# Two weight-split instructions pinned into a later place in their queues, at the end of the second block's output projection

## The chip, the cores and the metric

One core of a Trainium2 chip runs the whole program: two transformer blocks on 256 tokens of width 1024, batch 1, everything in fp32. The metric is the device time of one execution in microseconds (us); the number that counts is the median of the runs. Engines are named as in the profile: PE is TensorE, DVE is VectorE, ACT is ScalarE, POOL is GpSimd, SP is SyncE, which issues the loads.

## What is computed

The reference is two blocks in a row. The change lies in the second one, between its mixing part and its feed-forward part:

```python
mix = gates[:, :, 0] * y_attn + gates[:, :, 1] * y_pool + gates[:, :, 2] * y_mem
x = x + rms_norm(mix @ w_out[l], norm_mix_post[l])

h2 = rms_norm(x, norm_ffn_pre[l])
up = causal_depthwise_conv(h2 @ w_up[l], conv_w[l], conv_b[l])
g, v = jnp.split(up, 2, axis=-1)
ff = (jax.nn.gelu(g, approximate=True) * v) @ w_down[l]
x = x + rms_norm(ff, norm_ffn_post[l])
```

So after `mix @ w_out` each token row is normalised, added to `x`, normalised again, and only then can it meet `w_up`.

## The kernel before

**Products.** Every fp32 product is made of three: each operand is split into a high part `hi` (rounded to the matmul's format) and a remainder `lo`, and `mm3` (L205 to L208) sums hi·hi, hi·lo and lo·hi. In `b_part`, the form used here, the three matmuls on lines 206, 207 and 208 are x-hi with weight-hi, x-hi with weight-lo, x-lo with weight-hi, in this order.

**Weights.** All weights pass through one stream. A granule of 1 MB is loaded into one of three raw buffers (`feed`, L123) and is split in two halves by `split_next` (L129 to L151): ACT writes the half's `wh` by a cast (L142), then DVE, or POOL for one half that is marked so, writes `wl` by a subtraction (L143). There are six buffers of `wh` and six of `wl`; a half's buffers come free when PE has done the last matmul with it (`release`), a raw buffer when both halves' `wl` are written. `pump` splits one half ahead after each unit; `part` (L161 to L165) splits a half when its unit is reached and it isn't yet there.

**Order.** Only PE's queue follows the program text (`tc.manual_schedule` for PE). The queues of ACT, DVE, POOL and SP are ordered by the compiler's planner: an instruction that is not ready by the plan is passed by one that is. Each queue then runs in its order on the chip.

**The stage.** `out_stage` with `lead` set computes `mix @ w_out_2`. Tokens are two tiles of 128 rows, called t0 and t1 here; output columns are two halves, n0 and n1; w_out_2 is eight weight halves, four for n0 and four for n1. The last part is written out in `end_stage` and `close`:

- `first` (L505): `close(0)` does t0 with n1's four weight halves, splitting the last of them if need be; then t0's `finish`: add to `h`, squares on ACT, `pow` on POOL (L297), times the gain, and `scale` (L469 to L471), which multiplies x's columns 0 to 511 on DVE (L470) and the others on ACT (L471).
- `second` (L511): `close(1)` does t1 with n0's last two weight halves and n1's four. Ahead of the last of these it calls `turn` for t0: eight transposes on PE (L337), then `split_to`, which writes x^T's `hi` on ACT (L325) and `lo` on DVE (L326), in two column halves. Then comes t1's `finish`, with its own `scale`.
- `lead(0)` and `lead(1)` (L1307 on): the first matmuls with `w_up`, done in the row form so that they can start with one token tile. `lead(0)` takes t0 through six weight halves, called p0 to p5 here (`g_lead[0]` to `g_lead[2]`); t1's `turn` stands between p4 and p5. `lead(1)` takes t1 through the same six. p3's `wl` is on POOL, all others' on DVE.

No half of w_out_2 is left to be split after `close(0)`. So the first call of `split_next` after either `finish` is the one in `lead(0)` for p0. Behind p0 to p5, the next granule of the stream is the first of the feed-forward's own (p6, p7), which takes the raw buffer of p0 and p1.

Of the kernel before, what the change touches and what calls it, by code (L numbers as in the profile page):

```python
# [10 lines left out]
F32 = mybir.dt.float32  # L11
# [4 lines left out]
ALU = mybir.AluOpType  # L16
AX = mybir.AxisListType

P = 128
# [7 lines left out]
HALVES = (slice(0, 512), slice(512, D))  # L27
# [12 lines left out]
def two_blocks(ctx: ExitStack, tc: tile.TileContext, a: dict, out: bass.AP):  # L40
# [23 lines left out]
    V, S, G, PE = nc.vector, nc.scalar, nc.gpsimd, nc.tensor  # L64
# [3 lines left out]
    def nm(base):  # L68
        uid[0] += 1
        return f"{base}_{uid[0]}"  # L70
# [10 lines left out]
    XT, MT, ME = (xh, xl), (mh, ml), (eh, el)  # L81
# [7 lines left out]
    def s_t():  # L89
        return psum.tile([P, 512], F32, tag="s", name=nm("s"), bufs=4)  # L90
# [10 lines left out]
    def r32(ap):  # L101
        return ap.bitcast(F32R)
# [14 lines left out]
    def feed():  # L117
        while at_dma[0] < len(stream) and at_split[0] >= 2 * (at_dma[0] - N_RAW + 1):
            g = stream[at_dma[0]]
            g.raw = wraw.tile([P, g.nk, g.ncol], F32, tag="w", name=nm("w"))  # L120
            src = g.src.rearrange("(k p) c -> p k c", p=P)
            if at_dma[0]:
                nc.sync.dma_start(g.raw, src)  # L123
            else:
                for c in (slice(0, P), slice(P, 2 * P)):
                    nc.sync.dma_start(g.raw[:, :, c], src[:, :, c])
            at_dma[0] += 1

    def split_next(pieces=None, low=V):  # L129
        g, i = stream[at_split[0] // 2], at_split[0] % 2  # L130
        if g.by_col:
            c = g.ncol // 2
            src, shape = g.raw[:, :, i * c:(i + 1) * c], [P, g.nk, c]
        else:
            k = g.nk // 2
            src, shape = g.raw[:, i * k:(i + 1) * k, :], [P, k, g.ncol]
        hi = wspl.tile(shape, F32R, tag="wh", name=nm("wh"))
        lo = wspl.tile(shape, F32R, tag="wl", name=nm("wl"))
        g.parts[i] = (hi, lo)
        at_split[0] += 1  # L140
        if pieces is None:
            S.copy(hi, src)  # L142
            low.tensor_tensor(lo, src, hi.bitcast(F32), op=ALU.subtract)  # L143
        else:
            k = g.nk // 2
            for p in (np.s_[:, 0:k, :], np.s_[:, k:, :]):
                def piece(p=p):
                    S.copy(hi[p], src[p])
                    G.tensor_tensor(lo[p], src[p], hi[p].bitcast(F32), op=ALU.subtract)
                pieces.append(piece)  # L150
        feed()  # L151

    def pump(lead=N_SPLIT - 1):
        if at_split[0] < 2 * len(stream) and at_split[0] < n_used[0] + lead:
            split_next()

    def part(g, i, low=V):
        while g.parts[i] is None:
            assert at_split[0] < n_used[0] + N_SPLIT
            split_next(low=low)  # L160
        return g.parts[i]  # L161

    def release():
        n_used[0] += 1

    def place(fn, gran=None, pieces=()):

        if gran is not None:
            stream.append(gran)
        prog.append((fn, list(pieces)))  # L170
# [66 lines left out]
    def b_part(w, xt, t, k0, o, first, last):  # L237

        tok = slice(t * P, (t + 1) * P)
        for k in range(2):  # L240
            mm3(o, r32(xt[0][:, k0 + k, tok]), r32(xt[1][:, k0 + k, tok]), w[0][:, k, :], w[1][:, k, :],
                first and k == 0, last and k == 1)
# [24 lines left out]
    def ev_to(dst, scale=None):  # L267
        def ev(i, o):
            if scale is None:
                V.tensor_copy(dst, o)  # L270
            else:
                S.mul(dst, o, scale)
        return ev

    def grid(w, c0, n, dst, scale=None, xt=XT):

        u = []
        for g in range(n):
            u += a_units(cols(w, c0, g), xt, ev_to(dst[:, g * 512:(g + 1) * 512], scale))
        return u  # L280
# [40 lines left out]
    def split_to(dst, sl, src, scale=None):  # L321

        hi, lo = dst
        if scale is None:
            S.copy(r32(hi[sl]), src)  # L325
            V.tensor_tensor(r32(lo[sl]), src, hi[sl], op=ALU.subtract)  # L326
        else:
            S.activation(r32(hi[sl]), src, AF.Copy, scale=scale)
            V.scalar_tensor_tensor(r32(lo[sl]), src, scale, hi[sl], op0=ALU.mult, op1=ALU.subtract)  # L329

    def turn_rows(xn, t, dst, tile=tp_t):

        for c in range(2):
            o = tile()
            for k in range(4):
                kk = 4 * c + k
                PE.transpose(o[:, k * P:(k + 1) * P], xn[:, kk * P:(kk + 1) * P], ident)  # L337
            split_to(dst, np.s_[:, 4 * c:4 * c + 4, t * P:(t + 1) * P],
                     o.rearrange("p (k t) -> p k t", k=4))


    def turn_causal(pm):
# [48 lines left out]
    class Heads:  # L391


        def __init__(self, score, turn, pv):
            self.f, self.p, self.t = (score, turn, pv), {}, {}
# [17 lines left out]
    class Tail:  # L413
# [22 lines left out]
        def scale(self, dst, r):  # L436
            for n in range(2):
                V.tensor_scalar(dst[:, HALVES[n]], self.x[:, HALVES[n]], r[:, 0:1], None, op0=ALU.mult)
# [12 lines left out]
            self.scale(self.x, self.r)  # L451

        def turn(self):
            turn_rows(self.x, self.t, XT)

    class BlockEnd(Tail):

# [5 lines left out]
    class PostNorm(Tail):  # L463
# [3 lines left out]
            self.sum_times(self.o[n], n)  # L467

        def scale(self, dst, r):  # L469
            V.tensor_scalar(dst[:, HALVES[0]], self.x[:, HALVES[0]], r[:, 0:1], None, op0=ALU.mult)  # L470
            S.mul(dst[:, HALVES[1]], self.x[:, HALVES[1]], r[:, 0:1])  # L471

        def add(self, c):
# [22 lines left out]
    def end_stage(tails, close, fill, lead=None):  # L496


        def first():
            for _ in range(2):  # L500
                pump(N_SPLIT)
            close(0)()
            tails()[0].finish()

        def second():  # L505
            close(1)()
            tails()[1].finish()

        do(first)
        do(second)  # L510
        if lead is not None:  # L511
            lead(0, lambda: tails()[1].turn())
            lead(1, None)
        else:
            run(fill, {2 * t: [lambda t=t: tails()[t].turn()] for t in range(2)})

    def out_stage(src, xt, tail, gains, fill=(), at=None, lead=None):

        at = at or {}
        held = (2, 3) if lead is not None else ()  # L520
        st = {}
        gr = {(n, kq): Granule(src[kq * 512:(kq + 1) * 512, HALVES[n]], 4, 512, False)
              for n in range(2) for kq in range(2)}

        def unit0(i):
            if i == 0:
                st["o"] = [[s_t(), s_t()] for _ in range(2)]
                st["g"] = gains()
                st["tails"] = [tail(t, st["o"][t], st["g"]) for t in range(2)]
            w = part(gr[0, i // 2], i % 2)  # L530
            for t in range(1 if i in held else 2):
                b_part(w, xt, t, 2 * i, st["o"][t][0], i == 0, i == 3)
            if i not in held:
                release()
            if i == 3:
                for t in range(1 if held else 2):
                    st["tails"][t].half(0)

        for i in range(4):
            place(lambda i=i: unit0(i), gr[0, i // 2] if i % 2 == 0 else None, at.get(i, ()))  # L540
        stream.extend(gr[1, kq] for kq in range(2))

        def close(t):
            def go():
                for n, j in ([(0, j) for j in held] if t else []) + [(1, j) for j in range(4)]:
                    if held and (t, n, j) == (1, 1, 3):
                        st["tails"][0].turn()
                    b_part(part(gr[n, j // 2], j % 2), xt, t, 2 * j, st["o"][t][n], j == 0, j == 3)
                    if t == 1:
                        release()  # L550
                    if t == 1 and n == 0 and j == 3:
                        st["tails"][t].half(0)
                st["tails"][t].half(1)
            return go

        end_stage(lambda: st["tails"], close, fill, lead)
# [71 lines left out]
    def start():  # L628
# [53 lines left out]
        for _ in range(2):  # L682
            split_next(pieces)
        for p in pieces[0:2]:
            p()
        for k in range(8):
            split_to(XT, np.s_[:, k, :], o[k], g[:, k:k + 1])
            if k in (5, 7):
                pieces[k // 2]()
# [185 lines left out]
    def h_turn(c):  # L875
        def go():
            o = tp_t()
            for j in range(4):
                PE.transpose(o[:, j * P:(j + 1) * P], at_c(c)[:, j * P:(j + 1) * P], ident)
            split_to(MT, np.s_[:, 4:8, c * P:(c + 1) * P], o.rearrange("p (k t) -> p k t", k=4), hgrn_g)  # L880
        return go
# [555 lines left out]
```

## Time and profile before

| | us |
|---|---|
| median of 3 runs | 913.73 |
| lowest, highest run | 913.08, 915.52 |
| the profiled execution, whole | 914.16 |
| its span from first to last instruction | 912.30 |
| PE busy in the span | 898.0 (98%) |
| DVE, ACT, POOL busy | 588.4, 488.8, 130.0 |

The profiled execution took 1.86 us around its span. All times in the rows are us from the span's start. PE is the engine that is almost always busy; the stage of the change lies at 700 to 740 us.

### The profile page before, as it was taken

How to read it: one execution, taken by the hardware profiler on the slowest of the kernel's cores; microseconds unless marked ns; L12 is line 12 of the kernel's file. 1: busy time of each engine (PE TensorE's matmuls, PEld its weight loads, DVE VectorE, ACT ScalarE, POOL GpSimd, SP SyncE). 2: the span in 40 equal slices, each digit the busy share in tenths (PEclk: the TensorE clock that was granted, in tenths of full speed). 3: DMA queues.
4: the chain of work that ended last, by engine and by line, in shares of the span. 5: the costliest groups of instructions: out<-in, count | busy, mean ns of one | idle time of the engine just before them, and what ended most of it. 6: DMA issues, size and time to landing. Idle time of an engine off the chain costs nothing.

```text
span 912.3 us, 15217 instructions
## 1 busy us (share of the span) xinstructions
PE 898.0 (98%) x6213; PEld 823.9 (90%) x6213; DVE 588.4 (64%) x858; ACT 488.8 (54%) x743; POOL 130.0 (14%) x141
## 2 busy tenths in 40 slices
PE   8999999999999999999999999999999999999997
PEld 7999898898899999999898899999998789999995
DVE  5778775755575444555776455776756777766664
ACT  6745753555455444444654545667443676555552
POOL 3102220000002111111104000221211201101101
PEclk9999999999999999999999999999999999999999
DMA  8776544543555555555374555434555455555531
GB/s 271 256 253 186 185 155 164 198 153 114 167 193 192 195 190 193 189 185 185 131 250 135 183 179 185 139 131 133 200 185 185 161 185 183 188 201 193 166 135 47
DMA packets 117972, 162.39 MB, mean 178 GB/s; under 512 B 3647, under 2 KB 90509, under 8 KB 117901
## 3 DMA queue, kind: packets, MB, share of 16 engines
q1 hardware_dynamic: 117901, 161.41, 53.4%
q8 instruction: 49, 0.80, 0.3%
q14 instruction: 22, 0.18, 0.1%
HBM read 160.34 MB, written 1.06 MB: 177 GB/s over the span
## 4 chain that ended last, share of the span: by engine, by line
PE 90%; DVE 4%; ACT 2%; DMA 2%; POOL 1%; issue 1%; SPq 0%; DVEq 0%; POOLq 0%; ACTq 0%
PE mm L206 19%; PE mm L207 19%; PE mm L208 19%; PE s L208 8%; PE s L206 8%; PE s L207 8%; DMA w<-in_w_in_dram 2%; PE s L792 1%; POOL sm L297 1%; DVE wl L143 1%; PE tp L1068 1%; PE s L1060 1%; PE tp L337 1%; ACT wh L142 1%; PE s L1212 1%
## 5 line engine op out<-in xcount | busy, mean ns | idle before, releaser
L143 DVE TENSOR_TENSOR wl<-w,wh 128x1024 fp32r<-128x1024 f32 (+1 forms) x283 | 355.4, 1261 | 182.4 <-ACT wh L142 180.8
L142 ACT CAST wh<-w 128x1024 fp32r<-128x1024 f32 (+1 forms) x284 | 296.1, 1048 | 306.0 <-PE mm L207 190.2
L206 PE MATMUL mm<-xh,wh 128*128 128x256 f32 x1120 | 317.8, 284 | 0.0
L207 PE MATMUL mm<-xl,wh 128*128 128x256 f32 x1120 | 313.9, 280 | 0.3
L208 PE MATMUL mm<-xh,wl 128*128 128x256 f32 x1120 | 313.3, 280 | 0.0
L206 PEld LDWEIGHTS mm<-xh,wh 128*128 128x128 f32 x1120 | 211.3, 189 | 3.9 <-issue 2.3
L207 PEld LDWEIGHTS mm<-xl,wh 128*128 128x128 f32 x1120 | 211.2, 189 | 2.0 <-DVE xl L329 0.7
L208 PEld LDWEIGHTS mm<-xh,wl 128*128 128x128 f32 x1120 | 211.3, 189 | 0.0
L206 PE MATMUL s<-wh,mh 128*128 128x512 f32 x176 | 69.8, 396 | 0.0
L207 PE MATMUL s<-wl,mh 128*128 128x512 f32 x176 | 69.0, 392 | 0.0
L208 PE MATMUL s<-wh,ml 128*128 128x512 f32 x168 | 66.1, 393 | 0.0
L297 POOL TENSOR_TENSOR sm<-sm,half 128x1 f32<-128x1 f32 (+2 forms) x24 | 20.3, 847 | 234.2 <-DVE sm L310 221.7
L1103 POOL TENSOR_TENSOR r<-r 128x512 f32<-128x512 f32 x16 | 25.3, 1583 | 148.6 <-ACT r L1101 148.6
L206 PE MATMUL mm<-eh,wh 128*128 128x256 f32 x160 | 45.7, 286 | 0.0
L207 PE MATMUL mm<-el,wh 128*128 128x256 f32 x160 | 44.8, 280 | 0.0
L208 PE MATMUL mm<-eh,wl 128*128 128x256 f32 x160 | 44.7, 280 | 0.0
L208 PE MATMUL s<-wh,mh 128*128 128x512 f32 x112 | 44.1, 393 | 0.0
L1362 POOL TENSOR_TENSOR r<-r 128x512 f32<-128x512 f32 x11 | 21.4, 1946 | 148.0 <-DVE r L1350 124.2
L206 PE MATMUL s<-wh,ml 128*128 128x512 f32 x104 | 40.9, 394 | 0.0
L207 PE MATMUL s<-wl,ml 128*128 128x512 f32 x104 | 40.7, 392 | 0.0
L207 PEld LDWEIGHTS s<-wl,mh 128*128 128x128 f32 x176 | 33.1, 188 | 6.9
L206 PEld LDWEIGHTS s<-wh,mh 128*128 128x128 f32 x176 | 33.1, 188 | 6.7
(273 smaller groups left out, 1377.7 us busy)
## 6 DMA issues: line engine op xcount, KB each, us to landing
w<-in_w_in_dram SPq DMA_DIRECT2D x39, 1024.0 KB
w<-in_w_dram SPq DMA_DIRECT2D x32, 1024.0 KB
w<-in_w_up_dram SPq DMA_DIRECT2D x22, 1024.0 KB
w<-in_w_down_dram SPq DMA_DIRECT2D x11, 1024.0 KB
w<-in_w_xkv_dram SPq DMA_DIRECT2D x8, 1024.0 KB
w<-in_w_out_dram SPq DMA_DIRECT2D x8, 1024.0 KB
w<-in_w_xq_dram SPq DMA_DIRECT2D x4, 1024.0 KB
w<-in_w_xo_dram SPq DMA_DIRECT2D x4, 1024.0 KB
```

The costliest lines, as they stand in the source:

```text
L142: S.copy(hi, src)
L143: low.tensor_tensor(lo, src, hi.bitcast(F32), op=ALU.subtract)
L206: PE.matmul(o, lh, rh, start=first, stop=False)
L207: PE.matmul(o, lh, rl, start=False, stop=False)
L208: PE.matmul(o, ll, rh, start=False, stop=last)
L297: G.tensor_tensor(r[:, :n], v[:, :n], half.to_broadcast([P, n]), op=ALU.pow)
L337: PE.transpose(o[:, k * P:(k + 1) * P], xn[:, kk * P:(kk + 1) * P], ident)
L792: PE.matmul(o, k_[:, x], q2, start=True, stop=True)
L1060: PE.matmul(s[:, t, :], xq[:, j, t * P:(t + 1) * P], xkT[:, j, :], start=(c == 0), stop=(c == 1))
L1068: PE.matmul(o[:, c * T:(c + 1) * T], xv[:, m, cs], pt[:, m, :], start=(m == 0), stop=(m == 1))
L1103: G.tensor_tensor(tt, ra, ra, op=ALU.mult)
L1362: G.tensor_tensor(yv, yg, yv, op=ALU.mult)
```

## The change

Two instructions are remembered in `pin`: DVE's half of `PostNorm.scale` under "V", and the last ACT instruction of t0's x^T (the `hi` of its second column half) under "S". The next split that `split_next` makes on its usual engines is tied behind them: its cast behind the one under "S", its `wl` behind the one under "V". The tie is one of order in the engine's queue alone; it adds no instruction and no semaphore. `scale` runs once for t0 and once for t1 and sets the same entry; an entry is taken out by the split that uses it.

```diff
+    pin = {}
+
+    def behind(eng, x):
+        if eng in pin:
+            tc.add_manual_dep(x.ins, pin.pop(eng).ins.name,
+                              mybir.DependencyInfo(mybir.DependencyClass.NoSync, mybir.DependencyReason.DATA),
+                              reason="pin")
 
     def split_next(pieces=None, low=V):
@@
         if pieces is None:
-            S.copy(hi, src)
-            low.tensor_tensor(lo, src, hi.bitcast(F32), op=ALU.subtract)
+            behind("S", S.copy(hi, src))
+            x = low.tensor_tensor(lo, src, hi.bitcast(F32), op=ALU.subtract)
+            if low is V:
+                behind("V", x)
@@ def split_to
         if scale is None:
-            S.copy(r32(hi[sl]), src)
+            x = S.copy(r32(hi[sl]), src)
             V.tensor_tensor(r32(lo[sl]), src, hi[sl], op=ALU.subtract)
         else:
...
+            return None
+        return x
@@ def turn_rows
-            split_to(dst, np.s_[:, 4 * c:4 * c + 4, t * P:(t + 1) * P],
-                     o.rearrange("p (k t) -> p k t", k=4))
+            x = split_to(dst, np.s_[:, 4 * c:4 * c + 4, t * P:(t + 1) * P],
+                         o.rearrange("p (k t) -> p k t", k=4))
+        return x
@@ class Tail
         def turn(self):
-            turn_rows(self.x, self.t, XT)
+            return turn_rows(self.x, self.t, XT)
@@ class PostNorm
         def scale(self, dst, r):
-            V.tensor_scalar(dst[:, HALVES[0]], self.x[:, HALVES[0]], r[:, 0:1], None, op0=ALU.mult)
+            pin["V"] = V.tensor_scalar(dst[:, HALVES[0]], self.x[:, HALVES[0]], r[:, 0:1], None, op0=ALU.mult)
             S.mul(dst[:, HALVES[1]], self.x[:, HALVES[1]], r[:, 0:1])
@@ def close, in out_stage
                     if held and (t, n, j) == (1, 1, 3):
-                        st["tails"][0].turn()
+                        pin["S"] = st["tails"][0].turn()
```

## Rows read from the trace of the kernel before

**Rows 1.** The page: PE's busy time, and the chain's shares by engine.
```profile
PE 898.0 (98%) x6213; PEld 823.9 (90%) x6213; DVE 588.4 (64%) x858; ACT 488.8 (54%) x743; POOL 130.0 (14%) x141
...
PE 90%; DVE 4%; ACT 2%; DMA 2%; POOL 1%; issue 1%; SPq 0%; DVEq 0%; POOLq 0%; ACTq 0%
```

**Rows 2.** PE's waits, 705 to 740: who for whom, us, times, longest.
```profile
PE tp L337 <- DVE r L470: 1.4, 1, 1.4
PE mm L206 <- ACT xh L325: 0.5, 1, 0.5
```

**Rows 3.** Timeline of PE, 695 to 740: start, us, line, count [idle before <-releaser].
```profile
716.02 0.40 PE L208 MATMUL s<-wh,xl 128*128 128x512 f32 x1
716.91 0.50 PE L206 MATMUL mm<-wh,xh 128*128 128x512 f32 x1 [0.49 <-ACT xh L325]
717.24 0.40 PE L207 MATMUL mm<-wl,xh 128*128 128x512 f32 x1
717.63 0.50 PE L208 MATMUL mm<-wh,xl 128*128 128x512 f32 x1
...
723.77 0.40 PE L207 MATMUL s<-wl,xh 128*128 128x512 f32 x1
724.00 0.40 PE L208 MATMUL s<-wh,xl 128*128 128x512 f32 x1
725.75 1.06 PE L337 MATMUL tp<-ident,r 128*128 128x128 f32 x8 [1.35 <-DVE r L470]
```

**Rows 4.** Timeline of ACT, 690 to 745.
```profile
707.25 0.60 ACT L304 ACTIVATE junk<-s 128x512 bf16<-128x512 f32 x1 [4.84 <-PE s L208]
708.64 1.05 ACT L142 CAST wh<-w 128x1024 fp32r<-128x1024 f32 x1 [0.70 <-PE s L208]
...
714.39 1.98 ACT L142 CAST wh<-w 128x1024 fp32r<-128x1024 f32 x2
716.27 1.07 ACT L325 CAST xh<-tp 128x512 fp32r<-128x512 f32 x2
717.23 1.07 ACT L142 CAST wh<-w 128x1024 fp32r<-128x1024 f32 x1
...
718.66 0.22 ACT L304 ACTIVATION_READ_ACCUMULATOR junk<-s 128x1 f32 x1
...
729.64 1.05 ACT L142 CAST wh<-w 128x1024 fp32r<-128x1024 f32 x1 [2.15 <-PE mm L208]
```

**Rows 5.** Timeline of DVE, 690 to 745.
```profile
711.52 1.22 DVE L143 TENSOR_TENSOR wl<-w,wh 128x1024 fp32r<-128x1024 f32 x1
713.19 0.49 DVE L470 TENSOR_SCALAR r<-r,sm 128x512 f32<-128x512 f32 x1 [0.46 <-POOL sm L297]
...
718.33 1.68 DVE L143 TENSOR_TENSOR wl<-w,wh 128x1024 fp32r<-128x1024 f32 x1 [0.15 <-ACT wh L142]
719.93 0.20 DVE L310 TENSOR_SCALAR sm<-sm 128x1 f32<-128x1 f32 x1
...
725.12 0.49 DVE L470 TENSOR_SCALAR r<-r,sm 128x512 f32<-128x512 f32 x1 [0.45 <-POOL sm L297]
```

**Rows 6.** Timeline of SP's loads, 712 to 717; then busy times, clock, DMA, GB/s, 715 to 720.
```profile
714.84 0.37 SPq L123 DMA_DIRECT2D w<-in_w_up_dram  x1
...
715.00:720.00 5.00, 4.51 (x19) 3.06 (x18) 4.60 (x6) 4.82 (x8) 2.48 (x1) 1.00 0.66 211
```

**Rows 7.** The span's end: busy PE, PEld, DVE, ACT, POOL; PEclk, DMA, GB/s.
```profile
904.00:906.00 2.00, 1.68 (x8) 1.02 (x6) 0.41 (x1) 0.22 (x1) 0.00 (x0) 1.00 0.41 136
906.00:908.00 2.00, 0.00 (x0) 0.00 (x0) 1.44 (x4) 0.97 (x3) 0.56 (x2) 0.97 0.00 0
908.00:909.00 1.00, 0.00 (x0) 0.00 (x0) 1.00 (x2) 0.00 (x0) 0.84 (x1) 0.50 0.25 85
```

**Rows 8.** The same 128x128 weight load (ns min/median/max), first and last start us.
```profile
L642 PEld LDWEIGHTS mm<-ident x24: 287/333/333, 1.3 to 6.2; 128*128 128x128 f32 x24
...
L669 PEld LDWEIGHTS s<-ident,r x12: 138/140/143, 7.1 to 10.9; 128*128 128x128 f32 x12
```

## Prediction

> **What bounds the kernel now.** The page comes first: PE is busy for 98% of the span and carries 90% of the chain that ended last [rows 1]. The reader is to see that there is next to nothing to win outside PE's waits, and that any new wait of PE goes into the time in full. The second view is PE's waits in the stage of the change: only two, 0.49 us for t0's x^T ahead of the first lead matmul and 1.35 us for t1's scaling ahead of t1's transposes [rows 2]. The timeline of PE shows where they lie. These matmuls run in a pipeline, so I count by starts: in an undisturbed stretch of this form one starts 0.23 us behind the other (723.77, 724.00). By that, the product that starts at 716.02 is over at 716.25, line 207 could have started at 716.48 and started at 717.24 (0.76 lost); line 208 followed after 0.39 (0.16 lost, x^T's lo); the last of p4 is over at 724.23 and the transposes start at 725.75 (1.52 lost) [rows 3]. All the waits together are 2.4 us, 0.27% of the time. The last views are the timelines of ACT and DVE, read for who stands ahead of whom.
>
> **Which instructions are pinned.** The change has no arithmetic, only an order, so the whole forecast hangs on which split takes the pins. All eight halves of w_out_2 are split by the end of close(0), before either tile's finish. t0's scale sets the DVE pin; no split follows; t1's scale sets it anew; then lead(0) asks for p0. So p0's cast goes behind t0's second x^T hi on ACT, and p0's lo behind **t1's** scaling on DVE, not t0's. p0 is the very first weight half that lead(0) needs: PE's second lead matmul, line 207 at 717.24, reads p0's lo [rows 3]. And PE's order is fixed by the text: nothing behind this matmul can pass it.
>
> **ACT's part.** p0's cast now starts at 708.64, and the x^T hi pair ends at 717.34 [rows 4]. Behind it the cast takes 1.05 us, so it ends at about 718.3, in the place where p4's cast stands now (717.23). If p1 to p4 are not held up too, they take the places of p0 to p3 and ACT's timeline is a permutation; if they queue behind p0, ACT is empty at 714.39 and the x^T hi comes up to 1.9 us earlier. Either way PE's first lead matmul (line 206) moves from 716.91 to at most some 718.4. That is 1.5 us, but it is inside the next wait and costs nothing of its own.
>
> **DVE's part, the main term.** t1's scaling now runs from 725.12 to 725.61, and p0's lo takes 1.22 us [rows 5]. Unchanged otherwise, p0's lo would end at 726.84. It will be somewhat earlier: t1's chain of squares, sums and pow lost time behind p4's lo, which held DVE from 718.33 to 720.01 while the sum of squares was there at 718.88 (the read at 718.66 plus 0.22) [rows 4, 5]; the next step could start only at 719.93. With p0 in p4's place that gap on DVE stands empty, since p0's lo may not go there. I give the chain these 1.05 us back: scaling ends at 724.56, p0's lo at 725.8. The lower bound is the pace of t0's chain, which had free engines: from 707.25 to its scaling's end at 713.68 is 6.43 us [rows 4, 5]; t1's last product ends at 716.25 [rows 3], so its scaling can't end before 722.7 and p0's lo not before 723.9. The upper bound is 726.84. I take 725.8, since the one delay that I can name goes and the others stay.
>
> **What PE loses.** From line 207 at 717.24 to the end of p4's matmuls at 724.23 are 6.99 us, of which 0.16 was a wait: 6.83 us of work [rows 3]. New: line 207 starts at 725.8, the work ends at 732.6, t1's transposes follow at once, because t1 is by then long scaled. Now they start at 725.75 [rows 3]. The difference is 725.8 + 6.83 - 725.75 = **6.9 us** (bounds 5.0 and 7.9). All three waits of before are gone in this sum: they are swallowed by one wait of about 7.4 us, from the end of line 206 near 718.4 to 725.8. Behind t1's transposes the order is as before, everything shifted by the same amount; what had cover (x^T of t1 behind p5) keeps it.
>
> **What else moves.** On ACT the t1 chain, p5's cast and later work stand behind p0's cast, as they stood behind p4's: nothing. On POOL p3's lo may come a place earlier: nothing waits for it. On SP the load of the next granule (p6, p7) waits for the lo of p0 and p1; it was issued at 714.84 and its 1 MB (211 GB/s over 5 us) went within 715 to 720 [rows 6]. It will be issued at about 725.9, with two later loads and a gain row behind it in SP's queue, and land 5 us later, near 731. p6's cast stood at 729.64, released by PE [rows 4], and moves with PE to about 736 or later: some 5 us of cover. Nothing; if that cover were gone, each us past it would come on top.
>
> **PE's clock.** A wait of 7.4 us is longer than any that the trace has inside its work; the longest here is 1.35 us [rows 2]. What a long one does can be read at the span's end: PE's last matmul ends at 905.68 (1.68 us busy of 904 to 906), the mean granted clock of 906 to 908 is 0.97, and of 908 to 909 it is 0.50 [rows 7]. So it fell from 2.4 to 1.2 GHz at about 907.9, 2.2 us after the last work. The way back is seen only at the start: there a weight load took 333 ns from 1.3 to 6.2 us, and 140 ns from 7.1 us on, for the same shape [rows 8]. The clock column has no fall there, but the loads do. The level changed between 6.2 and 7.1, so it is some 5.4 us of work at half the clock, half of which is lost: 2.7 us. I take this as the price (an estimate from rows 8), since it is the only row of a climb, with 0 as the other end.
>
> The Trainium skill, "TensorE: Matmul & The Clock Gate", section "Part 1: The HAM clock gate", says that the slow level is the default state and that activity releases it; this speaks against a change that makes PE wait. The trace agrees at both ends of the span [rows 7, 8]. By this rule the time is the forecast below; without it, it is the first rival.
>
> **The sum.** In the profiled execution: span 912.30 + 6.9 + 2.7 = 921.9, with 1.86 around it 923.8; that execution lies 0.43 over the median of the runs, so the forecast is 913.73 + 9.6 = **923.3 us**.
>
> **The rivals.**
> (1) The clock holds, or falls too late to matter: 913.73 + 6.9 = 920.6. For it: the wait might be cut to the lower bound. Against: even then it is about 5.5 us, over twice the 2.2 us of rows 7.
> (2) The change does not tie what I read: p0's lo goes behind t0's scaling (713.19 to 713.68), which it follows anyway once its cast is late. Then only the cast counts: it ends at 718.3, the lo at 719.6, PE reaches t1's transposes at 726.4, 0.7 us later than now; with ACT cleared early (x^T hi 1.9 us sooner) PE would be there at 724.5 and t1's scaling, done at 724.56, would end the wait: 1.2 us gained. Time 912.5 to 914.4. Against it: the second scale overwrites the first one's pin before any split.
> (3) Faster: the pins clear ACT and DVE for the two tiles' chains and p0 is still there in time, so all three waits go. That is 2.4 us, 911.3; it decides only if p0's lo can be done before PE reaches line 207 near 717, and the pin on DVE rules this out unless (2) holds as well. Even then it is within what a measurement can tell, for a gain over 0.3% (2.7 us, about what a measurement of this kernel can tell from no change) is more than all the waits of the stage.
>
> **How the numbers follow.** Forecast 0.78; (1) 0.12; (2) 0.07; (3) 0.03. Slower by over 0.3%: the first two, and a rest of (2), 0.91. Within 0.3%: (2) and most of (3), 0.08. Faster: 0.01. The range takes in the bounds of both unknowns: low 5.0 without the clock's part, 918.7; high 7.9 + 2.7 = 10.6, 924.3, and 0.7 for the spread of the runs, 925.0. What is left out are (2) and (3), 1 in 10, and the tails.
>
> **What would show it.** Right: on PE, one wait of 6 to 8 us between the first and the second lead matmul (line 207 released by DVE wl L143), no wait ahead of t1's transposes, and a granted clock of 0.5 in part of the 15 us behind it; on DVE, a wl directly behind the second L470; on SP, a load of w_up 10 us later than 714.84 in its place. Wrong: line 207 starting before 720, which means that another instruction was pinned; or no clock below 1.0, which takes off 2.7; or a wait of p6's cast for its load, which would add to the sum.

## The result and the profile after

| | before | after |
|---|---|---|
| median of 4 runs, us | 914.62 | 923.0 |
| lowest, highest run | 913.08, 915.72 | 921.76, 924.0 |
| the profiled execution's span | 912.30 | 922.2 |

The ratio is 1.0087 (95% interval 1.0070 to 1.0103): slower by 8.0 us of 914.62; the medians lie 8.4 us apart. The four runs before are the three from above and one more. Lines of kernel.py have moved: 142 and 143 (cast and subtraction of a weight half) are 151 and 152, 206 to 208 are 217 to 219, 297 is 308, 304 is 315, 310 is 321, 325 and 326 are 336 and 337, 337 is 350, 434 is 448, 470 is 484, 474 is 488.

The two profiled executions were apart before they came to the stage: PE's clock was down for a while near the start of this one. The mean granted clock from 10 to 15 us was 1.00 before and 0.56 after. The view by windows of the kernel before (columns as in [rows 7]):

```profile
10.00:15.00 5.00, 4.11 (x27) 3.50 (x28) 3.96 (x10) 4.27 (x11) 3.96 (x5) 1.00 1.09 347
```

and the same view of the changed kernel:

```profile
10.00:15.00 5.00, 3.31 (x14) 2.79 (x15) 4.40 (x8) 2.25 (x6) 2.30 (x3) 0.56 1.10 348
```

PE is 3.0 us behind the kernel before by 20 us. Of that, 1.1 come back at 470 us, where PE waited 0.8 us in the kernel before (for an ACT instruction that stood behind two casts of a late load) and does not wait here. So the last product with w_out_2 starts at 717.93 and not at 716.02 [rows 3]. The change lies behind both places. Times of the stage are therefore counted from a common point, most simply from t0's transposes to t1's. The kernel before has t0's at

```profile
713.99 1.03 PE L337 MATMUL tp<-ident,r 128*128 128x128 f32 x8
```

and t1's at 725.75 [rows 3], 11.76 us later; the changed kernel has them at 715.90 and 735.63 (PE's timeline below), 19.73 us apart. The stage is **7.97 us** longer. The two spans differ by 9.9 us: 1.9 ahead of the stage, 7.97 in it, and nothing behind it. The ratio, too, gives 8.0 us.

The two waits of [rows 2] have become these, in the view of who waited for whom on PE, 705 to 760:

```profile
PE mm L218 <- DVE wl L152: 8.1, 1, 8.1
PE mm L217 <- ACT wh L151: 0.3, 1, 0.3
```

PE's timeline, which answers to [rows 3], shows the place: the second lead matmul, 8.6 us behind the first. Behind it the matmuls start every 0.43 us until 730.79 and every 0.23 from there, and t1's transposes wait for nothing:

```profile
715.90 1.04 PE L350 MATMUL tp<-ident,r 128*128 128x128 f32 x8
...
717.93 0.40 PE L219 MATMUL s<-wh,xl 128*128 128x512 f32 x1
718.61 0.49 PE L217 MATMUL mm<-wh,xh 128*128 128x512 f32 x1 [0.28 <-ACT wh L151]
727.21 0.79 PE L218 MATMUL mm<-wl,xh 128*128 128x512 f32 x1 [8.11 <-DVE wl L152]
727.80 0.63 PE L219 MATMUL mm<-wh,xl 128*128 128x512 f32 x1
728.23 0.63 PE L217 MATMUL mm<-wh,xh 128*128 128x512 f32 x1
...
730.36 0.59 PE L219 MATMUL mm<-wh,xl 128*128 128x512 f32 x1
730.79 0.40 PE L217 MATMUL mm<-wh,xh 128*128 128x512 f32 x1
731.03 0.39 PE L218 MATMUL mm<-wl,xh 128*128 128x512 f32 x1
...
735.63 1.04 PE L350 MATMUL tp<-ident,r 128*128 128x128 f32 x8
```

The same stretch in the view by windows (the number behind POOL's is the granted clock): 0.53 over the wait, 0.65 over the first matmuls behind it, then 1.00:

```profile
720.00:728.00 8.00, 0.79 (x2) 0.70 (x3) 7.28 (x8) 5.82 (x10) 2.88 (x3) 0.53 0.21 66
728.00:732.00 4.00, 4.00 (x14) 3.10 (x13) 3.70 (x4) 0.00 (x0) 0.00 (x0) 0.65 0.62 197
732.00:760.00 28.00, 28.00 (x162) 24.39 (x161) 16.23 (x22) 17.82 (x24) 1.25 (x1) 1.00 0.68 235
```

ACT's timeline, which answers to [rows 4]: between t0's squares and its x^T there is no cast any more; all six follow x^T, p0 at 717.49, then p1 and p2, p3, and p4 and p5. With x^T, t1's second half of squares (718.44) has moved forward:

```profile
716.53 1.07 ACT L336 CAST xh<-tp 128x512 fp32r<-128x512 f32 x2 [1.62 <-PE tp L350]
717.49 1.06 ACT L151 CAST wh<-w 128x1024 fp32r<-128x1024 f32 x1
718.44 0.61 ACT L315 ACTIVATE junk<-s 128x512 bf16<-128x512 f32 x1
...
719.02 2.00 ACT L151 CAST wh<-w 128x1024 fp32r<-128x1024 f32 x2
...
722.19 1.03 ACT L151 CAST wh<-w 128x1024 fp32r<-128x1024 f32 x1
...
724.09 1.98 ACT L151 CAST wh<-w 128x1024 fp32r<-128x1024 f32 x2
```

The same squares in the kernel before:

```profile
718.18 0.61 ACT L304 ACTIVATE junk<-s 128x512 bf16<-128x512 f32 x1
```

DVE's timeline, which answers to [rows 5]: t1's chain runs without a weight half in it, then the scaling takes 2.56 us where it took 0.49, and behind it stand all five lo of DVE, p0's first:

```profile
719.18 0.21 DVE L321 TENSOR_SCALAR sm<-sm 128x1 f32<-128x1 f32 x1 [0.73 <-ACT junk L315]
719.31 0.68 DVE L448 TENSOR_TENSOR r<-s,g 128x512 f32<-128x512 f32 x1
720.05 1.42 DVE L488 SCALAR_TENSOR_TENSOR h<-r,sm,h 128x512 f32<-128x512 f32 x2
721.38 1.29 DVE L448 TENSOR_TENSOR r<-h,g 128x512 f32<-128x512 f32 x2
722.59 0.21 DVE L321 TENSOR_SCALAR sm<-sm 128x1 f32<-128x1 f32 x1
723.46 2.56 DVE L484 TENSOR_SCALAR r<-r,sm 128x512 f32<-128x512 f32 x1 [0.67 <-POOL sm L308]
725.95 5.75 DVE L152 TENSOR_TENSOR wl<-w,wh 128x1024 fp32r<-128x1024 f32 x5
```

POOL's timeline beside it: t1's second `pow`, then p3's lo, which lies over the scaling:

```profile
722.88 0.55 POOL L308 TENSOR_TENSOR sm<-sm,half 128x1 f32<-128x1 f32 x1 [2.86 <-DVE sm L321]
723.39 2.35 POOL L152 TENSOR_TENSOR wl<-w,wh 128x1024 fp32r<-128x1024 f32 x1
```

The same second `pow` in the kernel before took 1.47 us, with p5's lo on DVE from 723.46 to 724.68 beside it:

```profile
723.46 1.22 DVE L143 TENSOR_TENSOR wl<-w,wh 128x1024 fp32r<-128x1024 f32 x1
```

POOL's timeline of the kernel before, t0's second `pow` and then t1's:

```profile
711.68 1.48 POOL L297 TENSOR_TENSOR sm<-sm,half 128x1 f32<-128x1 f32 x1 [2.86 <-DVE sm L310]
...
723.62 1.47 POOL L297 TENSOR_TENSOR sm<-sm,half 128x1 f32<-128x1 f32 x1 [2.85 <-DVE sm L310]
```

Last, SP and the cover of p6: its load is issued at 728.36, 13.5 us later than in [rows 6] (11.6 from the common point), and its cast on ACT is still released by PE, as in [rows 4]:

```profile
728.36 15.27 SPq L123 DMA_DIRECT2D w<-in_w_up_dram  x4
```

```profile
739.48 1.05 ACT L151 CAST wh<-w 128x1024 fp32r<-128x1024 f32 x1 [2.14 <-PE mm L219]
```

### The profile page after: what moved, and what is told of

The parts are those of the page before. It is cut to its first block, busy times and chain, and to the rows that moved or that the text cites. A ratio compares the mean times of both kernels' runs of the same rounds, so it can differ in the third digit from the quotient of the medians.

```text
span 922.2 us, 15217 instructions
## 1 busy us (share of the span) xinstructions
PE 900.6 (98%) x6213; PEld 827.0 (90%) x6213; DVE 592.7 (64%) x858; ACT 489.1 (53%) x743; POOL 127.9 (14%) x141
## 3 DMA queue, kind: packets, MB, share of 16 engines
HBM read 160.34 MB, written 1.06 MB: 175 GB/s over the span
## 4 chain that ended last, share of the span: by engine, by line
PE 94%; DVE 2%; ACT 1%; issue 1%; POOL 1%; DMA 1%; SPq 0%; DVEq 0%; POOLq 0%; ACTq 0%
PE mm L217 20%; PE mm L218 20%; PE mm L219 20%; PE s L219 8%; PE s L217 8%; PE s L218 8%; PE s L806 1%; PE tp L350 1%; PE tp L1082 1%; PE s L1074 1%; DMA w<-in_w_in_dram 1%; PE s L1226 1%; POOL sm L308 1%; PE tp L360 1%; DVE wl L152 1%
## 5 line engine op out<-in xcount | busy, mean ns | idle before, releaser
L218 PE MATMUL mm<-wl,xh 128*128 128x512 f32 (+1 forms) x96 | 36.8, 383 | 8.1 <-DVE wl L152 8.1
```

What stands on the lines that cost most here:

```text
L218: PE.matmul(o, lh, rl, start=False, stop=False)
```

## The experiments

Six more kernels were run. The table has the ratio to the kernel before and, from each profile, the time from t0's transposes to t1's and its difference from 11.76 us. Each stage is that of one execution; each ratio is over all runs. The difference agrees with the ratio to within some 1.2 us. Counted on to the end of the span instead, it is the same to 0.2 us in all but one: with both ties on p2 and p5 it is +1.7 and not +0.78, since there the clock is still down during t1's transposes and the product behind them.

| kernel | ratio (95% interval) | stage, us | against before |
|---|---|---|---|
| after | 1.0087 (1.0070 to 1.0103) | 19.73 | +7.97 |
| only the cast tied | 1.0072 (1.0050 to 1.0094) | 18.22 | +6.46 |
| only the lo tied | 1.0107 (1.0092 to 1.0123) | 21.07 | +9.31 |
| after, PE kept busy | 1.0076 (1.0063 to 1.0090) | 18.18 | +6.42 |
| after, p3's lo on DVE | 1.0061 (1.0044 to 1.0079) | 18.50 | +6.74 |
| both ties, on p2 and p5 | 1.0003 (0.9993 to 1.0012) | 12.54 | +0.78 |
| one tie, on p5's lo | 0.9992 (0.9981 to 1.0002) | 10.86 | -0.90 |

**Only the cast is tied.** From the changed kernel, `scale` no longer sets the pin:

```diff
-            pin["V"] = V.tensor_scalar(dst[:, HALVES[0]], ...)
+            V.tensor_scalar(dst[:, HALVES[0]], ...)
```

> Only p0's cast is tied behind t0's x^T hi; p0's lo is free. Theory (the tie of the lo on DVE is what costs): PE's second lead matmul starts within 1 us of where it stands in the kernel before, counted from the last product with w_out_2; a second wait of some 2.7 us for p1's lo follows, because in the changed kernel's trace DVE has no room for it until t1's rows are multiplied by the gain. In all +1.5 us, about 915.5, ratio 1.001 to 1.003; no clock below 1.0 inside the span. Rival (holding the casts back on ACT is what costs): as the changed kernel, +8 us, ratio 1.009.

The first part came as expected: the second lead matmul starts at 717.95, 1.94 us behind the last product with w_out_2, against 1.22 before. The second part did not: the wait for p1's lo is 5.0 us, not 2.7, the clock falls, and the time is +6.6 us, not +1.5. The rival's time is nearer (its 1.009 lies inside the interval), and it is right that holding casts back on ACT is dear; but it is not p0 that is late, since p0 is in time. PE's, DVE's and POOL's timelines of this kernel show the two causes:

```profile
717.95 0.50 PE L218 MATMUL mm<-wl,xh 128*128 128x512 f32 x1 [0.76 <-DVE wl L152]
...
724.64 0.79 PE L218 MATMUL mm<-wl,xh 128*128 128x512 f32 x1 [5.04 <-DVE wl L152]
```

```profile
720.01 3.44 DVE L448 TENSOR_TENSOR r<-h,g 128x512 f32<-128x512 f32 x2
723.37 1.21 DVE L152 TENSOR_TENSOR wl<-w,wh 128x1024 fp32r<-128x1024 f32 x1
```

```profile
720.13 2.77 POOL L152 TENSOR_TENSOR wl<-w,wh 128x1024 fp32r<-128x1024 f32 x1 [1.49 <-ACT wh L151]
```

p1's cast stands behind p0's on ACT, so DVE comes to p1's lo only after t1's additions and products; and the products (1.29 us for two elsewhere) take 3.44 while POOL writes p3's lo beside them. That POOL is the reason was tried for the scaling alone, below; for the products it is argued from that. Why the planner keeps the halves in order was not tried. So a tie on p0's cast alone is nearly as dear as both, by way of the halves behind p0.

**Only the lo is tied.**

```diff
-                        pin["S"] = st["tails"][0].turn()
+                        st["tails"][0].turn()
```

> Only p0's lo is tied behind t1's scaling; the casts are free. Theory (the tie on DVE): one wait of 8 to 10 us ahead of the second lead matmul, clock 0.5 for some 10 us, +8 to +10 us, about 922 to 924, ratio 1.008 to 1.011. Rival (the casts on ACT): PE starts the second lead matmul where it does before, ratio 1.000.

As the theory had it: one wait of 9.4 us, and +9.8 us. The intervals of this kernel and the changed one overlap; by the stage it is 1.34 us dearer than both ties together. Of this, 0.7 is t1's second half of squares, which comes later because ACT's casts lie in front of it again (1.24 us behind the last product's start and not 0.51), and 0.6 is the clock, which stayed down longer here. p3's cast is done by 717.7 in this kernel, and yet POOL writes p3's lo only at 724.46: the tie on p0's lo held back the lo of all six halves, on POOL too.

```profile
728.27 0.80 PE L218 MATMUL mm<-wl,xh 128*128 128x512 f32 x1 [9.38 <-DVE wl L152]
```

The two ties don't add up: either one alone makes PE wait for t1's chain, through p0's lo or through p1's.

**PE kept busy over the wait.** In `lead`, ahead of the first matmul:

```diff
+                    if t == 0 and (c, i) == (0, 0):
+                        o = tp_t()
+                        for _ in range(34):
+                            PE.matmul(o, r32(eh[:, 0, 0:P]), r32(eh[:, 0:2, :]), start=True, stop=True)
```

> The changed kernel with 34 idle-work matmuls (128x512, written to a spare PSUM tile that nobody reads) on PE ahead of the first lead matmul, some 7.8 us at 0.23 us each, so that PE is busy while it would wait. Theory (the fallen clock is 1.7 us of the loss): the granted clock stays 1.0 from 700 to 760 us, the matmuls behind the wait start every 0.23 us and not every 0.43, and the time is 1.7 us under the changed kernel's, +6.3 over before, ratio about 1.007. Rival (the clock costs nothing that counts, the loss is the wait alone): ratio 1.009 as the changed kernel.

By windows, the clock stays at 1.00 through the stretch in which it was 0.53 and 0.65:

```profile
717.00:725.00 8.00, 8.00 (x37) 6.50 (x35) 6.53 (x10) 7.76 (x13) 3.47 (x3) 1.00 0.20 66
725.00:735.00 10.00, 9.01 (x44) 7.25 (x43) 6.42 (x8) 1.73 (x4) 0.00 (x0) 1.00 0.64 209
```

The stage is 1.55 us shorter than the changed kernel's, with p0 as late as there (the second lead matmul starts 9.33 us behind the last product with w_out_2, against 9.28); the medians, 921.48 and 923.0, are 1.5 apart. That gives the clock's share in the changed kernel's profile: some 1.6 us. The intervals of the two ratios overlap; it is the windows and the stage that carry this.

**p3's lo on DVE.**

```diff
-                    b_part(part(g_lead[2 * c + i // 2], i % 2, G if (c, i) == (0, 3) else V), XT, ...
+                    b_part(part(g_lead[2 * c + i // 2], i % 2), XT, ...
```

> The changed kernel, with p3's lo on DVE and not on POOL. In the changed kernel's trace t1's scaling on DVE took 2.56 us where it takes 0.49 in the kernel before, while POOL wrote p3's lo (723.39 to 725.74). Theory (the two engines can't both read SBUF then, and the scaling waited for POOL): the scaling takes 0.49 again, p0's lo ends 2.1 us sooner, PE's wait is 6.0 us and not 8.1, and the time is 2.1 us under the changed kernel's: +5.9 over before, ratio about 1.0065. Rival (the scaling is long for another reason, such as the load on SBUF from ACT): it stays at 2.56 us, ratio 1.0087.

The scaling takes 0.49 again and the wait is 6.0 us:

```profile
722.83 0.49 DVE L484 TENSOR_SCALAR r<-r,sm 128x512 f32<-128x512 f32 x1 [0.66 <-POOL sm L308]
```

```profile
724.51 0.79 PE L218 MATMUL mm<-wl,xh 128*128 128x512 f32 x1 [6.03 <-DVE wl L152]
```

So POOL's writing of p3's lo was the reason for the 2.56 us. Of the 2.1 us saved in the wait the stage shows only 1.2: in this execution the clock stayed down longer behind the wait (matmuls 0.43 us apart from 724.51 to 729.8, against 727.21 to 730.8).

**Both ties on halves that are needed late.** p2's cast behind t0's x^T hi, p5's lo behind t1's scaling, by a condition on the number of the split (220 is p0):

```diff
-        if eng in pin:
+        if eng in pin and at_split[0] - 1 >= {"S": 222, "V": 225}[eng]:
```

> The same two ties on other halves: the cast of p2 (not p0) behind t0's x^T hi, the lo of p5 (not p0) behind t1's scaling. Theory: the ties are harmless, and useful, when the half is needed late: x^T of t0 comes some 1.8 us sooner on ACT, t1's second pow runs without p5's lo beside it (0.55 us, not 1.47), so PE's three waits of 2.4 us shrink to under 0.7; 1.7 to 2.3 us faster than before, ratio 0.9975 to 0.998. Rival (any tie of this kind delays the stage): ratio 1.002 or more.

Half of it came as expected: PE goes from w_out_2 into the lead without a wait, and t1's second `pow` takes 0.55. But the gain is not there: the ratio is 1.0003, and its interval holds neither the gain of the theory nor the rival's loss. DVE's and POOL's timelines show what took it:

```profile
718.19 3.54 DVE L488 SCALAR_TENSOR_TENSOR h<-r,sm,h 128x512 f32<-128x512 f32 x2
...
722.87 1.21 DVE L152 TENSOR_TENSOR wl<-w,wh 128x1024 fp32r<-128x1024 f32 x1
```

```profile
718.13 2.40 POOL L152 TENSOR_TENSOR wl<-w,wh 128x1024 fp32r<-128x1024 f32 x1
```

p3's cast queues behind p2's tied one, so p3's lo now falls beside t1's two additions, which take 3.54 us instead of 1.41; the chain is late by that, p4's lo with it, and PE waits 1.9 us for p4's lo:

```profile
724.13 0.50 PE L218 MATMUL s<-wl,xh 128*128 128x512 f32 x1 [1.89 <-DVE wl L152]
...
726.04 1.91 PE L350 MATMUL tp<-ident,r 128*128 128x128 f32 x8
```

In this execution the clock fell behind that wait, from about 724.6 to 728.0, and t1's transposes took 1.91 us where they took 1.06:

```profile
724.00:726.00 2.00, 1.87 (x5) 1.39 (x6) 1.34 (x4) 0.72 (x1) 0.55 (x1) 0.65 0.43 167
726.00:728.00 2.00, 2.00 (x10) 1.95 (x9) 0.72 (x2) 0.59 (x2) 0.00 (x0) 0.50 0.13 30
```

**One tie, on p5's lo alone.** Same condition, with the cast's number out of reach (999).

> One tie alone, where it should do no harm: p5's lo behind t1's scaling; all else as in the kernel before. Theory: t1's second pow on POOL, 1.47 us in the kernel before with p5's lo on DVE beside it, takes 0.55, and PE's wait for t1's scaling falls from 1.35 to some 0.4 us: 0.9 us faster, ratio 0.999, within what the times can tell. Rival (the pow's length has nothing to do with DVE): 1.47 stays, the wait stays, ratio 1.000.

The `pow` takes 0.55, PE's wait for t1's scaling goes from 1.35 to 0.46, and the stage is 0.90 us shorter:

```profile
723.02 0.55 POOL L308 TENSOR_TENSOR sm<-sm,half 128x1 f32<-128x1 f32 x1 [2.86 <-DVE sm L321]
```

```profile
724.24 1.06 PE L350 MATMUL tp<-ident,r 128*128 128x128 f32 x8 [0.46 <-DVE r L484]
```

The ratio, 0.9992 with an interval that holds 1, cannot tell 0.9 us from nothing; the profile can. No kernel that was run beats the one before by a measurable amount.

## Why the prediction was right

The forecast was 923.3 us and the measurement 923.0, by the mechanism that was forecast: p0's lo behind t1's scaling, one long wait of PE, and a fallen clock. That the two numbers lie so close is in part luck. 9.6 us were forecast on top of 913.73 (6.9 for the wait, 2.7 for the clock); the stage has 7.97, some 6.3 and 1.6 to 1.7. The median before, with its fourth run, came out 0.9 higher than the one I started from.

**Which instructions are pinned: right.** p0's lo is the first weight half behind t1's scaling on DVE, and the second lead matmul waits for it and for nothing else. The runs with one tie each show that on p0 neither of the two is harmless, which the forecast did not need.

**ACT's part: right for p0, in the second of its two forms.** The casts of p1 to p5 queue behind p0's; x^T's hi comes 1.65 us sooner against the last product (1.40 us ahead of it and not 0.25 behind). The late cast of p0 costs nothing of its own behind the longer wait (0.28 us lie ahead of it). But the forecast made no use of the second form: it brings t1's squares forward by the same 1.65 us, and so moves the main term.

**The main term: about right by luck, two errors that cancel in part.** Counted from the last product's start, I had t1's scaling end after 8.54 us; it ended after 8.09. But it began after 5.53, 2.5 us earlier than I thought, and took 2.07 us too long. The step that failed first is the chain's pace: I gave back only the 1.05 us that p4's lo had cost, and the chain also got 1.65 us from ACT (t1's second half of squares at 0.51 us behind the last product's start, 2.16 before) and 0.92 us from POOL, whose second `pow` was not slowed by a lo on DVE. My lower bound, the pace of t0's chain, was no free pace: t0's second `pow` had p0's lo beside it [rows 5] and took as long, 1.48 us. The run with p3's lo on DVE has the scaling done 6.0 us behind the last product, below that bound of 6.7. The step that failed second is the price of the scaling, taken as 0.49 wherever it stands; with POOL at work beside it, it is 2.56. It goes back to "On POOL p3's lo may come a place earlier: nothing waits for it": p3's lo came later, at 723.39, and the scaling on DVE did wait for it.

**What PE loses: right in kind.** All the waits of before are gone in one, 8.1 us where I had about 7.4 (the first lead matmul was earlier than I had it; a wait of 0.28 us lies ahead of it). The work behind it was as forecast, less the clock.

**The clock: right in kind, too dear.** It fell in the wait, from 2.4 to 1.2 GHz (granted 1.00, then 0.50), as the row of the span's end said it might. The price is read off PE's timeline: from 727.21 to 730.79 eight starts take 3.58 us, where eight times 0.23 are 1.85; 1.73 us lost, against 2.7. About 0.1 of it is the wider first gap that a start behind a wait has at the full clock too, as in the run in which PE is kept busy. The one climb that I had, at the start of the span, was longer than this one. The price differs from one execution to the next: by the same count, the runs with one tie on p0 and the one with p3's lo on DVE lost 2.2 to 2.5 us. Rival (1), without the clock, would have been +6.9 us; the run in which PE is kept busy is at +6.9 by its ratio and +6.42 in the stage, and its granted clock stays at 1.00. The rule of the Trainium skill that I set beside it ("TensorE: Matmul & The Clock Gate", "Part 1: The HAM clock gate"), that the slow level is the default and activity releases it, agrees in kind with these two traces: 0.53 over the wait, 1.00 where PE was kept busy.

**SP: right.** The load of p6 and p7 went out late and still landed under cover.

**A rival that was wrong.** Rival (2) priced the tie of the cast at -1.2 to +0.7 us, by looking at p0 alone. The run with only the cast tied costs 6.6. The working left out that p1 to p5 are held back as well, that their lo then meet t1's chain on DVE, and that the wait this makes brings the clock down (some 2.2 us of the cost).

## What to carry to other kernels

Before tying an instruction, ask who reads its result first and what that reader's queue holds behind it: the ties on p0 cost 8 us, the tie on p5's lo cost nothing. A result that is needed late is not enough, as the tie on p2's cast shows. In every kernel with a tied cast, all casts behind it in the stream were held back too; ask what follows the tied one. And a moved instruction has to be priced with its new neighbours: the same scaling was 0.49 or 2.56 us here, depending on what POOL did at that moment.

## What the runs showed of the hardware

DVE and POOL stopped each other in this stage. Beside POOL's subtraction (2.35 to 2.77 us), DVE's instructions with operands in SBUF took 2.56 instead of 0.49 (the scaling), 3.44 instead of 1.29 (two products) and 3.54 instead of 1.41 (two additions), each about 2.1 us more, whichever of the three it met. The other way round, `pow` on 128x1 took 1.47 beside a subtraction on DVE and 0.55 alone. For the scaling and for `pow` a run took the other engine's subtraction away and the long time went with it; the products and the additions were only seen side by side with it. The x^T lo of DVE, which read one operand from PSUM, ran beside POOL's subtraction in the kernel before at the 1.29 us for two that they take elsewhere. From DVE's and POOL's timelines of that kernel:

```profile
716.89 1.29 DVE L326 TENSOR_TENSOR xl<-tp,xh 128x512 fp32r<-128x512 f32 x2 [0.20 <-ACT xh L325]
```

```profile
716.45 2.48 POOL L143 TENSOR_TENSOR wl<-w,wh 128x1024 fp32r<-128x1024 f32 x1 [3.29 <-ACT wh L142]
```

The Trainium skill, "SBUF — State Buffer", section "Who interferes with whom", has this as a rule: DVE and GpSimd share a pair of SBUF ports by an exclusive lock, taken by DVE instructions with two SBUF inputs (against GpSimd instructions that read SBUF) or in a two-port mode. The numbers here agree with it.

The clock fell behind a shorter wait than I had expected: one of 1.9 us in the profiled execution with ties on p2 and p5, while the wait of 1.35 us in the kernel before left it at 1.00. The time from PE's last work to the fall was not the same each time: 1.4 us in the changed kernel, 4.6 in the run with p3's lo on DVE.
